# A state-space layer in a two-layer decoder trunk: issuing engines, order of loads and places of background products, on one core

## The chip, the core and the metric

The kernel runs on one core of a Trainium2 chip. A core has five engines that run side by side, each with its own instruction queue: TensorE (PE; its weight loads are shown as PEld), VectorE (DVE), ScalarE (ACT), GpSimd (POOL) and SyncE (SP), which here only issues DMA transfers. ACT and GpSimd can issue transfers too. An engine works its queue in order, so an instruction that waits holds up all that stand behind it. The metric is device time in microseconds of one execution; lower is better.

## The reference, cut to what matters

The model is a trunk of two layers for one sequence of 512 positions and 1024 channels in float32. Layer 0 mixes positions with attention, layer 1 with the state-space model below; each is followed by a gated feed-forward part. The shifts, scales and gates of every sub-layer come from a conditioning vector `c` by products with `w_mod`.

```
def s5_ssm(h, ...):                       # 64 groups of 16 channels, 64 complex states each
    u = h @ w_in
    bu = einsum('gph,bsgh->bsgp', b_bar, u in groups)
    _, states = associative_scan(combine, (lam_bar, bu), axis=1)   # over the 512 positions
    y = einsum('ghp,bsgp->bsgh', c_mat, states).real + d_skip * u
    z = gelu(y)
    g = z * sigmoid(z @ w_glu + b_glu)
    return g @ w_o
```

The result is multiplied by a gate and added to `x`; then comes a norm, whose shift and scale are again rows of `c_act @ w_mod + b_mod`.

## The kernel before

**Precision.** Matmuls run on pairs: a float32 tile is split into a rounded high half (a copy on ACT, `L163` for weights) and the remainder (a subtraction on VectorE, `L164`). `mm3` (`L169`, `L172`, `L173`) makes high x high, low x high and high x low, three matmuls for each 128x128 block of weights with 512 columns.

**Weights.** `load_w` takes 512 KB of weights from memory to a raw tile (three buffers, tag `wraw`), then splits it into one of `NW` = 5 pairs of buffers. The raw buffer comes free when the low half is made, the pair when the last matmul that reads it is done.

**Order of the instructions.** The program is written in one order, and a planner that estimates durations sets the order in each engine's queue when the kernel is built. Three things bind it: `tc.keep_in_program_order` (called `pe_pin` here, or `pinned=True` for gemvs) holds an instruction to the order of the program on its engine; `tc.issue_after` (in `behind_head` and `follow`) puts what is issued in a block behind a named instruction of the same engine; `follow("P", ...)` makes a chain of transfers on SP in this way. The planner also hands each transfer one of a small number of completion slots.

**Modulation in the background.** The 96 rows of the modulation are products of a 128x1024 piece of `w_mod` with `c_act` on VectorE (`gemv_step`, `L196`; its load on SP, `L195`, 512 KB into one of two `wg` buffers). Each is two rows of the profile, the product and a read of its accumulator. `bg(n)` issues the next `n`. Before the feed-forward part of layer 1 begins, all but the last 24 must be done; 18 are issued within the state-space layer.

**The state-space layer** (`ssm`). The 1024 channels are eight blocks of 128. For each block: eight units of `mm3` make `u` (`u_units`); ACT copies it to `ut` (`L1152`) and writes it to the DRAM tile `sU` (`L1153`, 256 KB in pieces of 256 bytes), from where it is read back in another layout as tile `u` (`L1155`). Four tables per block, made earlier, lie in DRAM: B (`pB`, 512 KB), R (`pR`, 256 KB), T and C (`pT`, `pC`, 512 KB each), with two buffers for each. `st_scan(bi)` multiplies `u` with B on PE (`pv`, 32 small matmuls), turns the result by R, scans it and turns it back on VectorE (eight to ten operations, `L1188` to `L1197`), and ACT copies the states to `st` (`L1202`). `st_out(bi)` makes `py` from u, T, `st` and C on PE (32 small matmuls) and ACT copies it to `yn` (`L1215`). `st_tr(bi)` transposes `yn` on PE (`pz`, `L1220`) and ACT applies gelu to give `z` (`L1223`).

A stage `s_` from 2 to 9 holds `st_out(s_-2)`, `st_scan(s_)` while there are blocks, two dense units, `st_tr(s_-2)`, and the rest of the dense units. The dense units are block 7 of `u` in stage 2, and then for each block `k` = `s_-3` the product of `z` of that block with the first five column blocks of `w_glu` (`glu_units`, weights `wglk`, 320 KB each), into five PSUM banks. PE's order here is that of the program.

After the stages PE makes the sixth column block (`g5`, weights `wgl`), the last block's units, and the seventh and eighth column blocks. Gating follows for each of the eight: sigmoid on ACT (`L1299`), times `z` on VectorE (`L1300`), split into `gzH` (ACT, `L1303`) and `gzL` (VectorE, `L1304`).

`out_proj` multiplies with `w_os`: two tiles are begun without the last of the eight gated blocks; the first five tiles are whole, each followed by its residual on VectorE (`L353`), a square on ACT (`L242`), a sum of squares on VectorE (`L243`) and the hook `after`; the last three tiles go in halves of 256 columns, and between the second halves PE makes the statistics of the first half (`stat`, `L264`) at a fixed place. In the same time the first four weights of the next part (`uph`) are loaded and split.

## Time and profile before

| | us |
|---|---|
| median of three timed runs | 1196.93 |
| their range | 1194.94 to 1197.47 |
| the profiled execution | 1194.65 |
| its span, first to last instruction | 1192.7 |
| its mean granted TensorE clock | 0.991 of full speed |

The profile is one execution on the chip. Its rows give the start in us, the duration, the engine, the line of the kernel, the operation and its tiles (output <- inputs), how many rows were merged, and in brackets how long the engine idled before it and what released it. A release is inferred; where the engine named had been done for long, it was something else, often a transfer. `SPq` and `ACTq` are issues of transfers. In the 10 us windows from 640 to 790 us, which hold the state-space layer, PE is busy for 8.8 to 10.0 of 10, VectorE for 4.4 to 9.4, ACT for 2.9 to 9.8, GpSimd for none, and the DMA engines for 0.20 to 1.03 of their time.

### The profile page before, as it was taken

What the parts mean: (1) busy time and instruction counts of PE and PEld (TensorE: products, weight loads), DVE (VectorE), ACT (ScalarE), POOL (GpSimd) and SP (SyncE); (2) the same over time, 40 slices, a digit from 0 to 9 for tenths busy, and PEclk for the clock granted to TensorE, in tenths of its full rate; (3) what the DMA queues carried; (4) which work ended last, traced back from release to release, by engine and by line L of the source; (5) the groups of instructions that cost most, each with busy time, mean ns of one, the idle gap of its engine ahead of it and who ended that gap; (6) DMA issues with size and microseconds to landing.
All of it is one profiled execution on the core that took longest, in us unless ns stands there. A gap on an engine that the chain in (4) does not pass through costs nothing.

```text
span 1192.7 us, 16459 instructions
## 1 busy us (share of the span) xinstructions
PE 1168.8 (98%) x6218; PEld 964.4 (81%) x6218; DVE 885.8 (74%) x1312; ACT 563.7 (47%) x893; POOL 270.4 (23%) x245
## 2 busy tenths in 40 slices
PE   8999999999999999989999999999999999999997
PEld 6887677699787878768889887879888888888887
DVE  6978988565999489888868598787598467744555
ACT  6756667456443134413336577646554134422443
POOL 1000000000298899998710000000000000000003
PEclk8999999999999999989999999999999999999999
DMA  8875653231348567778755598762166437442222
GB/s 301 316 262 165 203 179 109 90 121 54 89 142 273 177 215 222 207 233 294 247 153 182 182 322 288 246 224 77 53 216 225 124 118 188 153 124 71 83 76 71
DMA packets 92002, 211.00 MB, mean 177 GB/s; under 512 B 19602, under 2 KB 37906, under 8 KB 91923
## 3 DMA queue, kind: packets, MB, share of 16 engines
q1 hardware_dynamic: 83026, 205.76, 53.9%
q10 hardware_dynamic: 8320, 2.10, 0.8%
q0 software_dynamic: 576, 2.10, 0.5%
q8 instruction: 48, 0.79, 0.3%
q14 instruction: 32, 0.25, 0.1%
HBM read 188.68 MB, written 21.24 MB: 176 GB/s over the span
## 4 chain that ended last, share of the span: by engine, by line
PE 70%; POOL 8%; DVE 8%; DMA 7%; ACT 3%; issue 2%; SPq 1%; POOLq 0%; ACTq 0%; DVEq 0%
PE up L169 9%; PE up L172 9%; PE up L173 9%; PE dn L172 5%; PE dn L169 5%; PE dn L173 5%; PE o L772 2%; DVE ca L459 1%; PE t L754 1%; PE k L169 1%; PE q L169 1%; PE wo L169 1%; PE q L172 1%; PE q L173 1%; PE wo L173 1%
## 5 line engine op out<-in xcount | busy, mean ns | idle before, releaser
L173 PE MATMUL up<-hH,up_l 128*128 128x512 f32 x640 | 249.3, 390 | 1.1 <-DVE up_l L164 1.1
L169 PE MATMUL up<-hH,up_h 128*128 128x512 f32 x640 | 249.5, 390 | 0.0
L172 PE MATMUL up<-hL,up_h 128*128 128x512 f32 x640 | 249.3, 390 | 0.0
L459 DVE SCALAR_TENSOR_TENSOR ca<-up,small,ca 128x511 f32<-128x511 f32 (+1 forms) x176 | 131.4, 746 | 84.2 <-ACT ca L457 81.4
L196 DVE SCALAR_TENSOR_TENSOR wg<-wg,cact 128x1024 f32<-128x1024 f32 x96 | 122.8, 1294 | 40.1 <-DMA wg<-in_w_modT_dram 39.9
L172 PE MATMUL dn<-gL,dn_h 128*128 128x512 f32 (+1 forms) x394 | 145.9, 370 | 3.4 <-DVE gL L474 3.4
L169 PE MATMUL dn<-gH,dn_h 128*128 128x512 f32 (+1 forms) x394 | 146.3, 372 | 2.1 <-ACT gH L473 2.1
L173 PE MATMUL dn<-gH,dn_l 128*128 128x512 f32 (+1 forms) x394 | 145.7, 370 | 0.0
L173 PEld LDWEIGHTS up<-hH,up_l 128*128 128x128 f32 x640 | 120.1, 188 | 26.9 <-DVE up_l L164 2.0
L169 PEld LDWEIGHTS up<-hH,up_h 128*128 128x128 f32 x640 | 120.1, 188 | 26.0 <-issue 1.2
L172 PEld LDWEIGHTS up<-hL,up_h 128*128 128x128 f32 x640 | 120.1, 188 | 24.4
L1368 POOL TENSOR_SCALAR xa<-x,Anorm_out 128x256 f32<-128x256 f32 x7 | 5.7, 815 | 573.7 <-ACT dn_h L163 558.9
L163 ACT ACTIVATE up_h<-up_r 128x1024 fp32r<-128x1024 f32 x80 | 84.2, 1053 | 104.7 <-PE dn L172 48.0
L164 DVE TENSOR_TENSOR up_l<-up_r,up_h 128x1024 fp32r<-128x1024 f32 x80 | 121.9, 1524 | 10.1 <-ACT up_h L163 9.2
L457 ACT ACTIVATE ca<-up,small 128x512 f32<-128x512 f32 x88 | 67.7, 770 | 90.3 <-PE up L173 90.3
L172 PEld LDWEIGHTS dn<-gL,dn_h 128*128 128x128 f32 x394 | 75.1, 191 | 16.3 <-DVE gL L474 4.0
L169 PEld LDWEIGHTS dn<-gH,dn_h 128*128 128x128 f32 x394 | 75.0, 190 | 15.9 <-ACT gH L473 3.0
L173 PEld LDWEIGHTS dn<-gH,dn_l 128*128 128x128 f32 x394 | 75.0, 190 | 12.4
L353 DVE SCALAR_TENSOR_TENSOR x<-dn,mod,x 128x512 f32<-128x512 f32 (+1 forms) x55 | 37.3, 679 | 61.6 <-PE dn L173 61.6
L163 ACT ACTIVATE dn_h<-dn_r 128x1024 fp32r<-128x1024 f32 (+1 forms) x48 | 46.7, 981 | 55.9 <-PE dn L172 28.0
L466 ACT ACTIVATE ca<-ca 128x512 f32<-128x512 f32 x44 | 27.8, 632 | 91.7 <-DVE ca L459 89.9
L164 DVE TENSOR_TENSOR dn_l<-dn_r,dn_h 128x1024 fp32r<-128x1024 f32 (+1 forms) x48 | 62.8, 1308 | 8.3 <-ACT dn_h L163 8.1
(324 smaller groups left out, 2352.2 us busy)
## 6 DMA issues: line engine op xcount, KB each, us to landing
wg<-in_w_modT_dram SPq DMA_DIRECT2D x96, 512.0 KB
up_r<-in_w_up_dram SPq DMA_DIRECT2D x80, 512.0 KB
dn_r<-in_w_down_dram SPq DMA_DIRECT2D x32, 512.0 KB
wgs<-in_w_modT_dram SPq DMA_DIRECT2D x16, 512.0 KB
dn_r<-in_w_down_dram SPq DMA_DIRECT2D x16, 384.0 KB
wv_r<-in_w_v_dram SPq DMA_DIRECT2D x8, 512.0 KB
wk_r<-in_w_qk_dram SPq DMA_DIRECT2D x8, 512.0 KB
wq_r<-in_w_qk_dram SPq DMA_DIRECT2D x8, 512.0 KB
```

What stands on the lines that cost most here:

```text
L163: order("S", lambda: S.activation(wh[:, :n], raw[:, :n], AF.Copy))
L164: pin["split"] = order("V", lambda: V.tensor_tensor(wl[:, :n], raw[:, :n], wh[:, :n].bitcast(F32), ALU.subtract))
L169: ins = PE.matmul(ps, ah, bh, start=start, stop=False)
L172: PE.matmul(ps, ah, bl, start=False, stop=False)
L173: PE.matmul(ps, al, bh, start=False, stop=stop)
L196: mul = lambda: V.scalar_tensor_tensor(w, w, 1.0, cact, ALU.mult, ALU.mult, accum_out=raw[:, col:col + 1])
L353: add = lambda: V.scalar_tensor_tensor(xs, pv, gate, xs, ALU.mult, ALU.add)
L457: follow("S", lambda: S.activation(ca, ps, AF.Identity, bias=small[:, cb:cb + 1], scale=tapw[2]))
L459: follow("V", lambda: V.scalar_tensor_tensor(ca[:, q:], ps[:, :T - q], tapw[2 - q], ca[:, q:], ALU.mult, ALU.add))
L466: follow("S", lambda: S.activation(cg, cg, AF.Silu))
L754: ins = PE.transpose(pt[:, c:c + P], wts[pr][h2][i][:, j * P:(j + 1) * P], ident)
L772: ins = PE.matmul(po[pr][h2 * HD:(h2 + 1) * HD, j * P:], vn[:, j, hd:hd + HD], src, start=j == 0, stop=j == 3)
```

## The change

- The eight loads of `u` are issued by GpSimd instead of SP.
- The tables are asked for one by one (`load_tab`) in the chain on SP: in stage `s_` R of block `s_+1`, T and C of `s_`, B of `s_+2` (before: B and R of `s_+1`, then T and C of `s_`). The load of the GLU weights of block `s_-1` (`glu_load`) joins the chain behind them; before, the planner placed these loads. The weights of `g5` are loaded behind the last of the chain.
- The loads of `w_in` for blocks 4 to 7 stand together ahead of their units (`u_load`).
- Splitting `z` of block `s_-2` and the GLU weights of that block (`glu_split`) stands at the end of stage `s_`, with VectorE's two subtractions held to the program's order; before, it stood in stage `s_+1`, not held.
- A one-column gelu (`warm`) on ACT right behind the last norm tile brings the gelu table.
- Gemvs: three behind the last split of `w_in` ahead of the stages, two in stage 8 and one after stage 9 (before: four in each of the two, not held); none after the last two gating tiles (before: two after each); up to two instead of one behind each whole tile of the output projection.
- The gating tile `sg` has four buffers instead of two.
- `load_w` gets an argument `chain`, false by default.

```diff
-                def load_scan(bi):
-                    ...
-                def load_out(bi):
-                    ...
+                SRC = {"B": (sB, [P, 2, 512]), "R": (sR, [P, 2, 256]), "T": (sT, [P, 8, P]), "C": (sC, [P, 8, P])}
+                def load_tab(bi, which):
+                    for g in which:
+                        src, shape = SRC[g]
+                        if bi < 8:
+                            t = blk[bi][g] = tp.tile(shape, F32, tag="p" + g, bufs=2, name="p" + g)
+                            follow("P", lambda: SP.dma_start(t.rearrange("p r n -> p (r n)"), src[bi].rearrange("p r n -> p (r n)")))
...
-                    pin["u"] = SP.dma_start(u.rearrange("p g c -> p (g c)"), sU[bi].rearrange("j (h g) c -> h j (g c)", g=8))
+                    G.dma_start(u.rearrange("p g c -> p (g c)"), sU[bi].rearrange("j (h g) c -> h j (g c)", g=8))
+                warm = np_.tile([P, 64], F32, tag="warm", bufs=1, name="warm")[:, 0:1]
+                with behind_head():
+                    S.activation(warm, ones[:, 0:1], AF.Gelu_apprx_tanh)
...
+                def u_load(bi):
+                    with behind_head(pin["head"][HEADW[bi - 4]]):
+                        uw[bi] = load_w(I["w_in"][bi * P:(bi + 1) * P, :], name=f"win{bi}")
...
                 def glu_units(k):
-                    with behind_head([u_loads]):
-                        w = load_w(I["w_gluk"][k * P:(k + 1) * P, :], n=NGLU * P, name=f"wglk{k}")
+                    w = gw_[k][1:]
+                    dense.extend(...)
+                def glu_load(k):
+                    if k < KD:
+                        w = [wp.tile([P, D], F32R if g else F32, tag=("wraw", "wH", "wL")[g], bufs=NW if g else 3, name=f"wglk{k}_{g}")[:, :NGLU * P] for g in range(3)]
+                        follow("P", lambda: SP.dma_start(w[0], I["w_gluk"][k * P:(k + 1) * P, :]))
+                        gw_[k] = w
+                def glu_split(k):
                     S.activation(zh[0][k], zf[k], AF.Copy)
-                    V.tensor_tensor(zh[1][k], zf[k], zh[0][k].bitcast(F32), ALU.subtract)
-                    dense.extend(...)
+                    pe_pin(V.tensor_tensor(zh[1][k], zf[k], zh[0][k].bitcast(F32), ALU.subtract))
+                    raw, wh, wl = gw_[k]
+                    S.activation(wh, raw, AF.Copy)
+                    pe_pin(V.tensor_tensor(wl, raw, wh.bitcast(F32), ALU.subtract))
...
+                for bi in range(4, 8):
+                    u_load(bi)
                 u_units(4)
                 u_units(5)
+                with behind_head([pin["split"]]):
+                    bg(3, False)
                 run(UPRE)
                 st_scan(0)
-                load_scan(2)
+                load_tab(2, "BR")
                 u_units(6)
                 run(USTG[0])
                 st_scan(1)
+                load_tab(3, "B")
+                glu_load(0)
                 u_units(7)
                 run(USTG[1])
...
                     if s_ < 8:
                         st_scan(s_)
-                    if s_ + 1 < 8:
-                        load_scan(s_ + 1)
-                    if s_ < 8:
-                        load_out(s_)
+                        load_tab(s_ + 1, "R")
+                        load_tab(s_, "TC")
+                        load_tab(s_ + 2, "B")
+                    glu_load(s_ - 1)
...
                     st_tr(s_ - 2)
-                    if s_ >= 8:
-                        with behind_head([pin["comb"]]):
-                            bg(4, False)
+                    if s_ == 8:
+                        bg(2)
                     run(100)
-                gw, g5 = glu_w(NGLU), bank(aux, name=f"glu{NGLU}")
+                    if s_ == 2:
+                        zh = new_h()
+                    glu_split(s_ - 2)
+                    if s_ == 9:
+                        bg(1)
+                with behind_head([line["P"]]):
+                    gw = glu_w(NGLU)
+                g5 = bank(aux, name=f"glu{NGLU}")
...
-                sg = gp.tile([P, T], F32, tag="sg", bufs=2, name="sgl")
+                sg = gp.tile([P, T], F32, tag="sg", bufs=4, name="sgl")
...
-                if mt >= len(gb):
-                    bg(2)
...
-            R = out_proj(..., after=lambda: bg(min(1, sum(q[0] is not None for q in bgq) - 24)), ...)
+            R = out_proj(..., after=lambda: bg(min(2, sum(q[0] is not None for q in bgq) - 24)), ...)
```

More of the change, by code (lines that the diff above doesn't have):

```diff
@@ L142, in follow, with load_w @@
         return line[eng]
-    def load_w(src, n=D, name="w", own=None, lined=False):
+    def load_w(src, n=D, name="w", own=None, lined=False, chain=False):
         raw = wp.tile([P, D], F32, tag="wraw", bufs=3, name=name + "_r")
@@ L160, in load_w @@
             wl = wp.tile([P, D], F32R, tag="wL", bufs=NW, name=name + "_l")
-        pin["load"] = SP.dma_start(raw[:, :n], src)
+        fetch = lambda: SP.dma_start(raw[:, :n], src)
+        pin["load"] = follow("P", fetch) if chain else fetch()
         order = follow if lined else lambda eng, fn: fn()
@@ L1305, in ssm @@
                 gz.append((gh, gl))
[L1306 to L1307 removed]
             acc2 = new_acc()
[L1309 removed]
+            R = out_proj(lambda mt: I["w_os"][mt * P:(mt + 1) * P, :], gz, mcol(1, 2, 0), acc2, "wos", perm=True, after=lambda: bg(min(2, sum(q[0] is not None for q in bgq) - 24)),
                          head=([up_src(1, q, s) for q in range(2) for s in range(2)], "uph"))
```

25 lines of the change are left out of this document (6 added, 19 removed).

## The prediction

> **What bounds the kernel now.** I read the page first, then the TensorE waits, then TensorE's timeline through the state-space (SSM) layer. The page has TensorE (PE) busy for almost the whole span, so the change can only win what PE waits in the stages that it touches.
>
> ```profile
> span 1192.7 us, 16459 instructions
> PE 1168.8 (98%) x6218; PEld 964.4 (81%) x6218; DVE 885.8 (74%) x1312; ACT 563.7 (47%) x893; POOL 270.4 (23%) x245
> ```
>
> The span is 1192.7 us, that execution took 1194.65, and the median of the three timed runs is 1196.93. I count savings in the span and subtract them from the median; the executions shown differ by up to 2.5 us among themselves.
>
> In the stage loop each stage begins with the output products `py` of block s-2. The starts of stages 3 to 9, and of what follows the loop, are in PE's timeline (start, duration, operation):
>
> ```profile
> 702.59 1.09 PE L1146 MATMUL py<-pT,u 128*64 128x128 f32 x16
> ...
> 710.34 1.09 PE L1146 MATMUL py<-pT,u 128*64 128x128 f32 x16
> ...
> 717.26 1.09 PE L1146 MATMUL py<-pT,u 128*64 128x128 f32 x16
> ...
> 724.20 1.09 PE L1146 MATMUL py<-pT,u 128*64 128x128 f32 x16
> ...
> 732.47 1.09 PE L1146 MATMUL py<-pT,u 128*64 128x128 f32 x16
> ...
> 740.03 1.09 PE L1146 MATMUL py<-pT,u 128*64 128x128 f32 x16
> ...
> 747.53 1.09 PE L1146 MATMUL py<-pT,u 128*64 128x128 f32 x16
> ...
> 753.42 0.39 PE L169 MATMUL glu<-hH,wgl_h 128*128 128x512 f32 x1
> ```
>
> Stages 3 to 7 hold the same PE work. Stage 4 takes 717.26-710.34 = 6.92 and stage 5 takes 6.94: that is PE without a wait. Stage 3 takes 7.75 (0.83 over), stage 6 8.27 (1.35 over), stage 7 7.56 (0.64 over). Stages 8 and 9 have no scan products; stage 9 takes 5.89, stage 8 7.50 (1.61 over). The places of these waits, and the two of the output projection `wos`, with the idle time in brackets:
>
> ```profile
> 707.67 0.66 PE L1220 MATMUL pz<-consts,yn 128*128 128x128 f32 x4 [0.59 <-ACT yn L1215]
> ...
> 727.29 1.15 PE L1146 MATMUL pv<-u,pB 128*64 128x64 f32 x32 [1.12 <-DVE wgl_l L164]
> ...
> 744.85 0.66 PE L1220 MATMUL pz<-consts,yn 128*128 128x128 f32 x4 [1.24 <-ACT yn L1215]
> ...
> 776.76 0.39 PE L172 MATMUL wos<-gzL,wos_h 128*128 128x512 f32 x1
> 776.99 0.39 PE L173 MATMUL wos<-gzH,wos_l 128*128 128x512 f32 x1
> 777.56 0.49 PE L169 MATMUL wos<-gzH,wos_h 128*128 128x512 f32 x1 [0.19 <-ACT gzH L1303]
> 778.93 0.50 PE L172 MATMUL wos<-gzL,wos_h 128*128 128x512 f32 x1 [0.88 <-DVE gzL L1304]
> ```
>
> Without a wait, matmuls start 0.23 apart (the first two `wos` rows); the next two start 0.57 and 1.37 apart, so 0.34 + 1.14 = 1.48 is lost. All together 0.83 + 1.35 + 0.64 + 1.61 + 1.48 = **5.91 us** can be won, and no more.
>
> **The change part by part.** *Gelu's table.* ACT loads it inside stage 2, and runs late from there to the `yn` that stage 3 waits for:
>
> ```profile
> 700.37 1.28 ACT L1223 ACT_TABLE_LOAD   x1
> ...
> 707.02 0.60 ACT L1215 ACTIVATE yn<-py 128x512 f32<-128x512 f32 x1
> ```
>
> The load goes behind the last norm tile, where ACT idles until u0 is complete. 1.28 against a wait of 0.83: the wait goes, +0.83. No other table is needed between (ACT only copies there).
>
> *Order of loads; u off SP.* In stage 6 `pv` is released by no VectorE result (`wgl_l` is no input of it); its table B, row 721.73, was issued late. SP stood still before it:
>
> ```profile
> 705.46 0.37 ACTq L1153 DMA_DIRECT2D sU<-ut  x1
> ...
> 712.05 0.58 SPq L1128 DMA_DIRECT2D pT<-sT  x1
> 720.85 0.32 SPq L1128 DMA_DIRECT2D pC<-sC  x1
> ...
> 721.73 0.38 SPq L1121 DMA_DIRECT2D pB<-sB  x1
> ...
> SPq L1128 <- DMA sU<-ut: 8.2, 1, 8.2
> ```
>
> The load of pC shares no data with the write of sU, issued at 705.46; SP waited 8.2 us for that write all the same, as for a completion slot in use. Everything behind (B, the rotation table R, u) then came in one burst, so stages 6 and 7 waited, stage 7's scan came late, and stage 8 with it. In the new order B is asked for one stage earlier, u takes no place in SP's queue, and six of the eight GLU loads no longer crowd in ahead of the write. The slot itself stays: C of stage 4 is still about the eighth transfer after the last sU write, so the wait shrinks and does not go. B of block 6 follows it directly. Before, that load took 727.29 - 721.73 = 5.6 to arrive, and `pv` of stage 6 will be due at 724.20 - 0.83 + 2 = 725.4; so the write has to be done by some 719, two us sooner than before. I think it is, and credit 1.35 + 0.64 = 1.99 of stages 6 and 7.
>
> *VectorE's order in a stage; z and weight splits behind the scan.* The scan's end, and so ACT's `st`, comes one subtraction earlier. In stage 8 `yn` stood right behind this row, which ends at 744.18:
>
> ```profile
> 742.50 1.68 ACT L1202 ACTIVATE st<-m 64x252 f32<-64x252 f32 x4 [1.27 <-DVE m L1197]
> ```
>
> 1.61 goes, but stage 8 has no `pv` to cover the split of block 5, now due behind the scan: at most one subtraction, 0.60 by the row of acc below; taken 0.3. The loads of w_in for blocks 4 to 7, listed earlier, were done by then anyway: nothing. `chain` in `load_w` is used by nobody: nothing. The first of the last three GLU weights is now loaded behind the last table, where its low half was made in stage 6 before (`wgl_l` at 727.29). Its buffer comes free with the split of block 5, early in stage 8, so from 740.03 - 2.82 = 737.2 to some 740; PE needs it when stage 9 ends, 753.42 - 4.43 = 749.0. Load and split have 9 us: hidden, with a few us to spare.
>
> *u by GpSimd.* The nearest price is GpSimd's own transfer of sR in an earlier phase (issue 0.8 us, 512 KB each; u has 256), against u0's issue and the first scan product:
>
> ```profile
> 678.96 4.56 SPq L1155 DMA_DIRECT2D u<-sU  x3
> ...
> 682.83 1.15 PE L1146 MATMUL pv<-u,pB 128*64 128x64 f32 x32
> ...
> DMA to landing us min/median/max: 3.4/3.5/4.3
> ...
> 684.03 0.69 DVE L1188 TENSOR_TENSOR m<-pv,pR 128x512 f32<-128x512 f32 x1 [6.76 <-PE pv L1146]
> ```
>
> 678.96 + 3.5 = 682.46 is in time, + 4.3 = 683.26 is 0.43 late; below, nothing is won, since PE did not wait. Taken 0.2. GpSimd's own queue is empty here, so nobody stands behind it; later u's have a stage or more. [...]
>
> *Three gemvs behind the last w_in split.* They take 1.14 each on VectorE (below) in the 6.76 that it idles, last row above; their three loads (1.5 MB) land among the first u transfers. Free while the first scan keeps its slack of several us; taken 0.3 for the shared DMA.
>
> *Gating.* Four gemvs leave it, five leave stages 8 and 9, and four buffers let the sigmoids run ahead: the 1.48 goes.
>
> *Output projection.* Eighteen gemvs must be done before the next layer's modulation; 2+3+2+1 are placed earlier, so ten stay for five tiles, two behind each tile. Before, the window held eight (x16 counts accumulator reads too), four of them ahead of the first residual:
>
> ```profile
> 766.00:812.00 46.00, 9.79 (x16) 1.00 0.70 226
> ...
> 784.29 1.23 DVE L196 SCALAR_TENSOR_TENSOR wg<-wg,cact 128x1024 f32<-128x1024 f32 x1 [2.51 <-DMA wg<-in_w_modT_dram]
> ...
> 786.98 1.28 DVE L353 SCALAR_TENSOR_TENSOR x<-wos,mod,x 128x512 f32<-128x512 f32 x1
> ...
> 804.13 0.69 DVE L243 TENSOR_TENSOR acc<-acc,sq 128x512 f32<-128x512 f32 x1
> 804.73 1.22 DVE L196 SCALAR_TENSOR_TENSOR wg<-wg,cact 128x1024 f32<-128x1024 f32 x1
> ...
> 805.87 1.18 DVE L353 SCALAR_TENSOR_TENSOR x<-wos,mod,x 128x512 f32<-128x512 f32 x1
> 806.97 1.22 DVE L164 TENSOR_TENSOR uph_l<-uph_r,uph_h 128x1024 fp32r<-128x1024 f32 x1
> ...
> 812.73 0.42 DVE L243 TENSOR_TENSOR acc<-acc,sq 128x256 f32<-128x256 f32 x1 [0.54 <-ACT sq L242]
> ...
> 785.00 0.39 PE L173 MATMUL wos<-gzH,wos_l 128*128 128x512 f32 x1
> ...
> 813.53 0.50 PE L264 MATMUL stat<-ones,acc 128*128 128x1 f32 x4
> ...
> 820.76 0.28 PE L173 MATMUL up<-hH,uph_l 128*128 128x256 f32 x1
> ```
>
> The last sum of squares ends at 813.15 and `stat` on PE, whose place is fixed, starts 0.38 later: VectorE is the close second here. PE has tile 0 at 785.00 + 0.39 = 785.4, so VectorE may use 813.53 - 785.4 = 28.1. It will need ten gemvs at 1.14 (804.73 to 805.87), 11.4; five residuals at 1.10 (805.87 to 806.97), 5.5; four sums at 0.60, 2.4; three splits of `wos` and four of `uph` at 1.2, 8.4; and for the three last half tiles a residual and a sum each, some 1.0 by the row of 0.42, 3.0. That is 30.7: 2.6 too many. A split of `uph` whose buffer comes late falls behind `stat`; with one or two of them 1.4 or 0.2 remain. Ends: 0.2 and 2.6, more if loads are late (rivals). I take **1.5 us of new PE wait before `stat`**.
>
> Sum: 5.91 - 0.3 - 0.2 - 0.3 - 1.5 = 3.6, so a span of 1189.1 and a median of **1193.3**.
>
> **The rivals.** (1) *VectorE fits*: the `uph` splits fall behind `stat`, no new wait; 5.91 - 0.8 = 5.1, 1191.8. For it: PE uses them from some 820 on (row 820.76). Against: they are ready at the same time.
>
> (2) *The stages stay late*: the sU write holds SP as long as before, and only the table and gating terms come, 0.83 + 1.48 less 1.5: 0.8, 1196.1. For it: the same eight-transfer distance, and 1.5 MB of gemv loads moved ahead of it. Against: less is queued.
>
> (3) *Slower*: the gemvs are kept behind the sums before them, and each pair has its loads issued only when the pair before is done. The row at 784.29 waited 2.51 for such a load. If two of the four later pairs wait so, VectorE is 2.6 + 5.0 = 7.6 late at `stat`: 5.1 - 7.6, 1199.4. It decides once the wait before `stat` is over 5.1.
>
> [...]
>
> (5) *Not as said*: what is not pinned is ordered by the planner's clock, and new order elsewhere eats the gain: 1196.9.
>
> **How the numbers follow.** Forecast 0.45 (own range 1191.3 to 1195.0), (1) 0.17, (2) 0.17, (3) 0.13, (4) 0.03, (5) 0.05. A measurement tells about 0.2% (2.4 us) from no change. Faster: most of the forecast (0.37), all of (1), a little of (2), 0.57. Slower: most of (3) and little else, 0.13. Same: 0.30. The range 1190.2 to 1199.0 takes in (1) with the spread of runs and reaches into (3).
>
> **What would show it.** Right: stages 3 to 7 all near 6.92, stage 8 near 6.2, no table load after 690, no SP wait of 8 us for sU, no wait at the first `wos` tile, a wait of 0.2 to 2.6 before `stat` that VectorE's sum releases. Wrong: `pv` of block 0 waiting for u by over 0.5; the g5 products waiting for wgl5; `stat` more than 3 late, or not at all.

## The result and the profile after

| | before | after |
|---|---|---|
| median of the timed runs, us | 1197.15 (4 runs) | 1210.56 (4 runs, 1206.63 to 1214.04) |
| ratio after / before, with 95% interval | | 1.0119 (1.0092 to 1.0146) |
| profiled execution, us | 1194.65 | 1206.63 |
| its span, us | 1192.7 | 1204.5 |

The changed kernel is 1.2% slower. The forecast was 1193.3 us with a range up to 1199.0; the time lies 11.6 us above that range. Line numbers of the changed kernel differ by a few from those of before; the names are the same.

TensorE's waits within the state-space layer (what waited <- what ended it: us in all, times, longest):

```profile
PE glu L174 <- DVE wgl_l L165: 3.5, 1, 3.5
PE stat L265 <- DVE acc L244: 3.3, 1, 3.3
PE pv L1143 <- issue: 2.6, 1, 2.6
PE glu L170 <- ACT wgl_h L164: 0.4, 1, 0.4
PE glu L174 <- DVE wglk L1263: 0.2, 1, 0.2
...
PE pz L1221 <- ACT yn L1216: 0.2, 1, 0.2
```

The waits of before that the prediction counted are gone or down to 0.2: those for `yn`, for B and for `gz`. (The row left out is a wait of 0.2 for `hL` at the start of the layer, which both kernels have.) In their place stand three that before did not have, at `pv` of block 0, at the sixth GLU product and at `stat`: 2.58 + (0.44 + 3.53) + 3.31 = 9.9 us. The span grew by 11.8, although the stages became shorter, so the waits alone are not the whole loss. To see the rest, TensorE's timeline is cut at five landmarks: the statistics that open the layer, the first `py`, `pz` of block 7, the first product of `out_proj`, and the second `rbc` in it. Before, then after:

```profile
645.08 0.17 PE L264 MATMUL stat<-ones,acc 128*128 128x1 f32 x1
...
694.29 0.33 PE L1146 MATMUL py<-pT,u 128*64 128x128 f32 x2
...
750.91 0.27 PE L1220 MATMUL pz<-consts,yn 128*128 128x128 f32 x1
...
773.14 0.39 PE L169 MATMUL wos<-gzH,wos_h 128*128 128x512 f32 x1
...
827.71 0.38 PE L286 MATMUL rbc<-dg,ones 128*128 128x256 f32 x1
```

```profile
644.72 0.17 PE L265 MATMUL stat<-ones,acc 128*128 128x1 f32 x1
...
698.08 0.33 PE L1143 MATMUL py<-pT,u 128*64 128x128 f32 x2
...
752.09 0.27 PE L1221 MATMUL pz<-consts,yn 128*128 128x128 f32 x1
...
780.43 0.39 PE L170 MATMUL wos<-gzH,wos_h 128*128 128x512 f32 x1
...
839.49 0.38 PE L287 MATMUL rbc<-dg,ones 128*128 128x256 f32 x1
```

Segment by segment, after minus before: to the first `py` 53.36 - 49.21 = +4.15; the stage loop 54.01 - 56.62 = **-2.61**; the sixth GLU product and what follows 28.34 - 22.23 = +6.11; `out_proj` 59.06 - 54.57 = +4.49. Together +12.1. In each of the three segments that lost, the loss is larger than its wait. Why, the granted clock shows, in windows behind the three waits (PEclk is the third number from the end):

```profile
685.00:690.00 5.00, 4.88 (x42) 4.25 (x43) 2.83 (x6) 0.60 (x1) 1.04 (x2) 0.66 0.98 282
760.00:765.00 5.00, 5.00 (x15) 4.00 (x16) 2.21 (x2) 1.06 (x1) 0.00 (x0) 0.66 1.03 325
...
825.00:830.00 5.00, 5.00 (x29) 4.95 (x29) 1.46 (x5) 0.38 (x1) 0.00 (x0) 0.66 0.19 71
```

TensorE is busy in these windows and gets 0.66 of its clock; in before it is 1.00 in every window from 640 to 850 us. That is the second part of the loss: from the first `pv` to the second 6.89 - 5.39 = 1.50 us, behind the GLU product 6.11 - 3.97 = 2.1, at and behind `stat` 4.49 - 3.31 + 1.48 = 2.7 (the last with the 1.48 of the gating, which was won): some 6.3 us in all, in which the slower start behind a wait is counted too (the product behind the wait of 0.44 is followed 0.34 us later, that behind 3.53 after 0.38, where the others of the GLU product at full clock stand 0.23 apart). So the three places cost 9.9 + 6.3 = 16.2 us, and the stage loop and the gating won 4.1.

The stage loop did what was forecast for its first five stages:

```profile
706.38 1.09 PE L1143 MATMUL py<-pT,u 128*64 128x128 f32 x16
...
713.32 1.09 PE L1143 MATMUL py<-pT,u 128*64 128x128 f32 x16
...
727.18 1.09 PE L1143 MATMUL py<-pT,u 128*64 128x128 f32 x16
...
734.10 1.09 PE L1143 MATMUL py<-pT,u 128*64 128x128 f32 x16
...
741.07 1.09 PE L1143 MATMUL py<-pT,u 128*64 128x128 f32 x16
...
748.35 1.09 PE L1143 MATMUL py<-pT,u 128*64 128x128 f32 x16
...
754.59 0.39 PE L170 MATMUL glu<-hH,wgl_h 128*128 128x512 f32 x1
```

Stage 3 takes 6.94, stages 4 and 5 together 13.86, stage 6 6.92, stage 7 6.97. Stage 8 takes 7.28 (7.50 before) and stage 9 6.24 (5.89 before): nothing was won there.

### The profile page after: what moved, and what is told of

The parts are those of the page before. It is cut to its first block, busy times and chain, and to the rows that moved or that the text cites. A ratio compares the mean times of both kernels' runs of the same rounds, so it can differ in the third digit from the quotient of the medians.

```text
span 1204.5 us, 16456 instructions
## 1 busy us (share of the span) xinstructions
PE 1174.6 (98%) x6218; PEld 968.8 (80%) x6218; DVE 875.2 (73%) x1312; ACT 562.7 (47%) x894; POOL 273.4 (23%) x253
## 4 chain that ended last, share of the span: by engine, by line
PE 73%; POOL 10%; DVE 6%; DMA 4%; ACT 3%; issue 2%; SPq 0%; POOLq 0%; DVEq 0%; ACTq 0%
PE up L170 9%; PE up L173 9%; PE up L174 9%; PE dn L170 5%; PE dn L173 5%; PE dn L174 5%; PE o L773 2%; PE t L755 1%; PE k L170 1%; PE u L173 1%; PE u L170 1%; PE u L174 1%; PE q L170 1%; PE wo L170 1%; PE k L173 1%
## 5 line engine op out<-in xcount | busy, mean ns | idle before, releaser
L165 DVE TENSOR_TENSOR up_l<-up_r,up_h 128x1024 fp32r<-128x1024 f32 x80 | 114.5, 1431 | 15.4 <-ACT up_h L164 14.4
```

The source lines that it names most:

```text
L165: pin["split"] = order("V", lambda: V.tensor_tensor(wl[:, :n], raw[:, :n], wh[:, :n].bitcast(F32), ALU.subtract))
```

## The experiments

Each is the changed kernel with a small edit, but for e13, which is the kernel before. The ratio is to the kernel before, run on the same chip between them. The intervals of e1 to e6, each with two of the three losses or more left in, overlap with the changed kernel's, so there the segments of one profile carry the argument; those of e7, e8, e9 and e12 do not overlap with it. The four segments are those above, in us against before's first profile; a minus is a gain.

| | ratio (95%) | to first py | stage loop | GLU | out_proj | layer |
|---|---|---|---|---|---|---|
| the change | 1.0119 (1.0092 to 1.0146) | +4.1 | -2.6 | +6.1 | +4.5 | +12.1 |
| e1 u by SyncE | 1.0083 (1.0055 to 1.0110) | -0.1 | -2.6 | +7.0 | +5.0 | +9.3 |
| e2 early gemvs moved | 1.0101 (1.0059 to 1.0143) | +0.7 | -1.1 | +7.1 | +5.3 | +12.1 |
| e3 wgl5 first | 1.0069 (1.0044 to 1.0093) | +4.7 | -0.9 | 0.0 | +4.9 | +8.7 |
| e4 one gemv a tile | 1.0085 (1.0055 to 1.0114) | +6.4 | -2.4 | +7.5 | -1.7 | +9.8 |
| e5 gemvs without loads | 1.0108 (1.0085 to 1.0131) | -0.1 | 0.0 | +6.0 | +1.5 | +7.5 |
| e6 TensorE kept busy | 1.0105 (1.0074 to 1.0135) | +6.2 | -2.3 | +5.0 | +2.3 | +11.2 |
| e7 three mended | 1.0007 (0.9990 to 1.0024) | +0.2 | -1.4 | 0.0 | -0.7 | -1.9 |
| e8 same, u of 4 to 7 by GpSimd | 1.0013 (0.9995 to 1.0031) | +0.1 | -2.0 | 0.0 | +0.8 | -1.1 |
| e9 splits placed by hand | 1.0011 (0.9991 to 1.0030) | -0.1 | -0.8 | +1.6 | -1.7 | -0.9 |
| e10 gelu not ahead | one time | +6.7 | -2.5 | +6.9 | +4.9 | +15.9 |
| e11 two gating buffers | one time | +6.2 | -2.1 | +6.8 | +4.5 | +15.4 |
| e12 third gemv out | 0.9987 (0.9967 to 1.0007) | 0.0 | -3.4 | 0.0 | -1.0 | -4.4 |
| e13 before again | one time | 0.0 | -1.9 | 0.0 | +0.5 | -1.3 |
| e14 e12 again | one time | 0.0 | -1.9 | 0.0 | -1.5 | -3.4 |

The start of the layer lies between 641.85 and 649.28 us in these profiles, with no edit ahead of it; the kernel before alone has 645.08 and 647.59. That spread is in every time, and the segments are free of it.

### Who makes u late: e1, e2, e5

e1 undoes the issuing engine:

```
-                    G.dma_start(u..., sU[bi]...)
+                    SP.dma_start(u..., sU[bi]...)
```

> The changed kernel with one thing undone: SyncE issues the loads of u again, as before the change; the three early gemvs stay. In the changed kernel pv of block 0 waits 2.58 us for u and the landmarks of TensorE lose about 4 us there. Theory Q (the queue: GpSimd's path is what makes u late, 5.7 us from issue to landing for block 0): u of block 0 lands in 2 to 3 us, the wait at pv is under 0.5 us and 4 us come back; SyncE's wait for a slot behind the u loads returns and costs up to 2 us in stages 6 and 7, so 1206 to 1209 us. Theory C (contention: u's transfer shares the DMA engines with the gemv loads, whoever issues it): u still takes over 4 us from issue, the wait stays over 1.5 us, and the time is 1210 us or more with the slot wait on top (1212). The waits of 3.5 us ahead of the GLU product and 3.3 us ahead of the statistics stay under both.

`pv` of block 0 no longer waits, and the stage loop keeps all of its gain (-2.6). So taking u off SyncE is not what won in the stages: SyncE's longest wait of a table load for a write of `sU` is 1.7 us in e1, against 8.2 in before. That the new order of the table loads did it is argued and not shown, as no run undoes that order alone; and how much was won at all, e13 below puts in doubt. But e1 doesn't separate queue from contention, as its issues show. The changed kernel's and then e1's (start, time over the merged rows, queue):

```profile
678.08 1.49 SPq L196 DMA_DIRECT2D wg<-in_w_modT_dram  x2
...
679.37 1.16 POOL L1153 DMA_DIRECT2D u<-sU  x2 [77.60 <-DMA sU<-ut]
```

```profile
673.62 1.47 SPq L196 DMA_DIRECT2D wg<-in_w_modT_dram  x2
680.46 0.58 SPq L1153 DMA_DIRECT2D u<-sU  x1
681.13 0.54 SPq L196 DMA_DIRECT2D wg<-in_w_modT_dram  x1
```

In the changed kernel two gemv loads of 512 KB go out just ahead of u0 (two more had been used by then); in e1 the third goes out only behind u0, since both stand in one queue. The queue that u left had also kept gemv loads behind it.

e2 moves the gemvs and leaves u on GpSimd:

```
-                with behind_head([pin["split"]]):
-                    bg(3, False)
...
                 gz.append((gh, gl))
+                if mt >= 5:
+                    bg(1)
```

> The changed kernel with the three early gemvs moved to the gating (one after each of its last three tiles), u still loaded through GpSimd. Two gemv loads of 512 KB, those of stage 8, are still issued beside u's. Theory C (contention with the gemv loads): u of block 0 lands in about 3 to 4 us, pv waits under 1 us, and 3 to 4 us come back: 1206 to 1208 us. Theory Q (GpSimd's path): the landing stays near 5.7 us, the wait over 2 us, and the time within 1 us of the changed kernel's, 1210. A third theory, L (VectorE's multiplications of the gemvs hold up GpSimd's issue), gives what C gives here, and is told from it by a run that keeps the loads without the multiplications. The waits ahead of the GLU product and the statistics stay.

The wait fell to 0.68, and u0 landed 3.7 us after its issue began (5.7 in the changed kernel):

```profile
683.73 1.15 PE L1143 MATMUL pv<-u,pB 128*64 128x64 f32 x32 [0.68 <-issue]
```

No gemv load was issued in the 6 us before u0 here. Contention or VectorE, then. The layer as a whole gained nothing here: the stage loop gave back 1.5 (waits for `yn` of 1.4), and `stat` waited 4.3 in place of 3.3; neither was followed up. e5 lets VectorE multiply without the loads:

```
-                    bg(3, False)
+                    bg(3, False, load=False)      # multiplies cact by itself
```

> The changed kernel in which the three early gemvs multiply without their loads (the vector by itself, in place of the weights), so that three of the modulation values are not the reference's. VectorE does the same three multiplications at the same place; 1.5 MB of loads are gone. With those gemvs moved away altogether, u of block 0 landed 3.15 us after its issue ended (5.08 in the changed kernel) and pv waited 0.7 us (2.58). Theory C (the loads fill the DMA engines): the same here, a landing of 3.0 to 3.4 us, a wait under 1 us, the ratio to before about 1.010. Theory L (VectorE's multiplications hold GpSimd's issue or its descriptors): landing 4.5 us or more, wait 2 us or more, ratio 1.012.

u0 again landed in 3.7 us, and `pv` did not wait at all. All three multiplications stood beside the transfer here (679.54 to 683.05, the transfer from 679.68 to 683.4), more than in the changed kernel, where two were done before u0's issue. VectorE's multiplications are innocent; **the loads of the early gemvs made u late**, by 2.0 us (5.7 to landing), and in the other five profiles with u on GpSimd and these loads by more: 6.4 in e3 and e11, 6.5 in e4, 6.8 in e6 and 6.9 in e10, with waits at `pv` of 3.3 to 3.8. The changed kernel's own profile shows this loss at its smallest.

The rest of the 2.58, about what e2 still waits (0.68), comes ahead of the read. From the issue of the write to the issue of the read it took 679.37 - 673.77 = 5.60, and on SyncE in before 678.96 - 674.14 = 4.82. ScalarE waits for the same write, to use `ut` again, and so shows when it was done. Rows of after, then of before:

```profile
673.77 0.38 ACTq L1150 DMA_DIRECT2D sU<-ut  x1
...
678.88 0.60 ACT L1149 ACTIVATE ut<-u 128x512 f32<-128x512 f32 x1 [3.23 <-DMA sU<-ut]
```

```profile
674.14 0.38 ACTq L1153 DMA_DIRECT2D sU<-ut  x1
...
678.98 0.60 ACT L1152 ACTIVATE ut<-u 128x512 f32<-128x512 f32 x1 [2.96 <-DMA sU<-ut]
```

The read's issue on GpSimd comes 0.49 behind ScalarE's row, and on SyncE 0.02 ahead of it; e1 to e6, e10 and e11 have the same 0.49 or 0.02. The other 0.27 is the write's. In e5 the write, too, was done 2.4 us sooner (679.19 - 676.48 = 2.71), as no gemv loads stood ahead of it, so its missing wait is not the landing's alone.

e5's ratio is larger than its layer (+7.5 us) lets expect. Its profiled execution had a mean granted clock of 0.994, and the three others 0.990 or 0.991: they may have had the half clock behind `stat` that this one lacks (see the last section), but they left no profile.

### The sixth GLU weight: e3

The chain in the changed kernel, on VectorE's timeline, and the row of ScalarE's that it could have followed:

```profile
756.14 0.69 DVE L1260 TENSOR_TENSOR hL<-z,hH 128x512 fp32r<-128x512 f32 x1 [5.14 <-ACT hH L1259]
756.75 0.82 DVE L1263 TENSOR_TENSOR wglk<-wglk,wglk 128x640 fp32r<-128x640 f32 x1
757.49 1.22 DVE L197 SCALAR_TENSOR_TENSOR wg<-wg,cact 128x1024 f32<-128x1024 f32 x1
...
758.63 2.35 DVE L165 TENSOR_TENSOR wgl_l<-wgl_r,wgl_h 128x1024 fp32r<-128x1024 f32 x2
```

```profile
747.96 1.06 ACT L164 ACTIVATE wgl_h<-wgl_r 128x1024 fp32r<-128x1024 f32 x1
```

The low half of wgl5 is made at 758.63 on VectorE, though ScalarE (last row) had made its high half at 749.0. VectorE idled for 5.14 us in between, in front of hL of block 7, which is pinned to the program's order and waits for the last gelu; the last split of `wglk` and the gemv of stage 9 stood ahead of it too. e3 puts the split ahead of them:

```
+                    if s_ == 9:
+                        with behind_head([line["P"]]):
+                            gw = glu_w(NGLU)
                     glu_split(s_ - 2)
...
-                with behind_head([line["P"]]):
-                    gw = glu_w(NGLU)
```

> The changed kernel with the sixth GLU weight (wgl5) loaded and split ahead of the pinned splits of stage 9, not behind them. Theory O (order: its split on VectorE stands behind hL of block 7, which waits 5.14 us for its input, though its own input was there 9.6 us before): the waits of 0.44 and 3.53 us at the GLU product go, with the half clock behind them; the first product of out_proj comes 5 to 6 us earlier, and the time is 1204 to 1206 us. Theory D (VectorE is simply short of time there: the split only changes places with others that are needed as much): another wait of 2 us or more appears in stage 9 or ahead of the products of block 7, and the time stays above 1208 us. The waits at pv of block 0 and at the statistics stay under both.

The 6.1 us are gone, clock and all. Some 1.7 came back in the stage loop, 1.1 of it in stage 9, which is neither 0 nor theory D's 2. hH of block 6 began 2.1 us behind the end of the gelu that it needs (752.36 against 750.29), and in the changed kernel 1.0 (748.93 against 747.93): ScalarE's half of wgl5's split stood between in both, but in e3 it waited 0.49 for its load, and a split of `wglk` stood there as well. TensorE waited in many small steps:

```profile
PE glu L170 <- ACT hH L1259: 0.8, 2, 0.4
PE glu L174 <- DVE wglk L1263: 0.5, 2, 0.2
PE glu L173 <- DVE hL L1260: 0.4, 2, 0.2
```

### The pairs of gemvs: e4

```
-  after=lambda: bg(min(2, sum(...) - 24))
+  after=lambda: bg(min(1, sum(...) - 24))
...
-                        bg(1)            # stage 9
+                        bg(2)
+                if mt >= 6:              # gating
+                    bg(2)
```

> The changed kernel with one gemv after each of out_proj's first five tiles, as before the change, not two; the other five go to stage 9 (one) and to the last two tiles of the gating (two each). Theory G (the pairs of gemvs, each waiting for its 512 KB load, hold the residual sums and with them acc and the statistics): the wait of 3.31 us ahead of stat falls below 1 us, its half clock goes, and the time is 1204 to 1206 us; some 1.5 us may come back as a wait in the gating, as it was before. Theory R (the sums are late for another reason: weight splits on VectorE or the squares on ScalarE): stat still waits over 2 us and the time stays within 1.5 us of 1210. A fourth gemv in stage 9 may lengthen the wait at the GLU product by 1.2 us.

The wait at `stat` is gone, and `out_proj` is 1.7 us shorter than before's. In the changed kernel VectorE was full; from the first residual to the last sum that `stat` needs:

```profile
790.84 1.28 DVE L354 SCALAR_TENSOR_TENSOR x<-wos,mod,x 128x512 f32<-128x512 f32 x1 [6.12 <-PE wos L174]
...
819.53 1.23 DVE L197 SCALAR_TENSOR_TENSOR wg<-wg,cact 128x1024 f32<-128x1024 f32 x1 [1.09 <-DMA wg<-in_w_modT_dram]
...
821.01 1.22 DVE L197 SCALAR_TENSOR_TENSOR wg<-wg,cact 128x1024 f32<-128x1024 f32 x1
...
822.16 0.42 DVE L244 TENSOR_TENSOR acc<-acc,sq 128x256 f32<-128x256 f32 x1
```

That is 822.58 - 790.84 = 31.7 us with 1.09 of it a wait for a load. Behind 790.84 TensorE left 819.32 - 790.84 = 28.5 us for it, so VectorE was late by what it had too much, 2.2, and by that wait for a load, 1.09. The four gemvs in the gating cost no wait there, with four gating buffers; the gemv added to stage 9 (the fourth of stages 8 and 9) lengthened the GLU wait to 4.7, as expected.

### The clock: e6

```
+                for q in range(16):
+                    pe_pin(PE.matmul(g5, wk(gw, 0)[0], zh[0][0], start=True, stop=True))
...
+        for q in range(12):              # ahead of stat
+            pe_pin(PE.matmul(R["ps"][:, 256:256 + P], ones, ones, start=True, stop=True))
```

> The changed kernel with work that is thrown away put into two of TensorE's waits: 16 repeats of the sixth GLU product's first matmul (some 0.23 us each) ahead of the wait for the split of wgl5, and 12 matmuls of 128x128 into unused columns of the statistics' bank ahead of the wait for acc. Neither wait ends earlier by this. Theory H (the granted clock falls because TensorE was idle): the clock of 0.83 behind the first wait and of 0.66 behind the second become 1.00, the work behind them takes 1.6 to 2 us and 2.7 us less, so the ratio to before falls from 1.012 to about 1.008. Theory P (the clock falls for another reason, such as the load on the memory or on the other engines at that time): the clock stays under 0.9 in both windows, and the ratio at 1.012. The wait at pv of block 0, left as it is, keeps its half clock.

The clock stayed at full behind both places, where windows of this length had shown 0.66 (the wait at the GLU product ended at 767.29 here, that at `stat` at 828.80):

```profile
767.00:772.00 5.00, 4.71 (x21) 3.88 (x22) 2.59 (x3) 1.06 (x1) 0.00 (x0) 1.00 1.01 360
...
830.00:835.00 5.00, 5.00 (x42) 4.94 (x42) 3.38 (x13) 1.74 (x4) 0.00 (x0) 1.00 0.34 103
```

So in these two places the idle time is the cause of the half clock, not the other engines' load. `out_proj` took back 2.2 us, all of it behind `stat`; the GLU segment only 1.1, since the wait there, fillers and all, was 16 x 0.23 + 1.1 = 4.8 in this execution in place of 3.97. `pv`, left alone, waited 3.6 in place of 2.58 and kept its half clock, so the layer is only 0.9 us shorter than the changed kernel's. The ratio of 1.0105 does not tell theory H from theory P; the clock in the windows does.

### Are gelu's table and the buffers worth anything: e10, e11

```
-                with behind_head():
-                    S.activation(warm, ones[:, 0:1], AF.Gelu_apprx_tanh)      # e10
...
-                sg = gp.tile([P, T], F32, tag="sg", bufs=4, name="sgl")         # e11
+                sg = gp.tile([P, T], F32, tag="sg", bufs=2, name="sgl")
```

> The changed kernel without the instruction that has gelu's table loaded ahead. The prediction put 0.83 us of the stage loop to it. Theory T (the table load of 1.28 us is on the path at the first gelu): from the first py to the last pz the kernel is 1.6 to 2.0 us shorter than before's, in place of 2.62, and a wait of 0.8 us is back in stage 3. Theory F (the stages have slack there once tables and VectorE's work are in order): 2.3 us or more, no new wait. The three losses stay, so the single time says little: 1206 to 1214 us.

The table load is back inside stage 2, and the stage loop is as short as with it ahead: theory F, in one execution. Stage 3, from the `py` at 708.78 to that at 715.72, takes 6.94:

```profile
704.03 1.28 ACT L1221 ACT_TABLE_LOAD   x1
```

> The changed kernel with two gating buffers, as before the change; no gemv is in the gating in either. The prediction put the wait of 1.48 us at out_proj's first tile to the buffers and the four gemvs of the gating together. Theory B (the buffers): a wait of 1 us or more for gz is back at the first tile, and from there to the statistics the kernel loses that much against the changed one. Theory M (the gemvs in the gating were the cause): the wait is under 0.4 us. Its time says little: 1206 to 1214 us.

With two buffers, too, there is no wait for `gz` (theory M). With four buffers and four gemvs in the gating (e4) there is none either. Only with the two together, as in before, was the wait of 1.48 there, so either half of the change seems enough. In e4 and e11, though, TensorE had stood still for 4 to 5 us just ahead of the gating, which gave VectorE and ScalarE time. For the buffers, e7 and e12 below show the same without that pause (four buffers, gemvs in the gating, no wait for `gz`); for two buffers with no gemvs no run shows it.

### Mended together: e7, e8, e9, e12

e7 takes the edits of e1, e3 and e4, with five gemvs in the gating (1, 2 and 2 behind its last three tiles) in place of the one more in stage 9.

> The changed kernel with the three places mended together: u issued by SyncE, wgl5 loaded and split ahead of the splits of stage 9, one gemv after each of out_proj's first five tiles and five gemvs after the last three tiles of the gating. If the three losses are separate and their mends add up (0.36, 0.50 and 0.34% of the time when done singly, the last with 1.2 us more from a gemv that is not added to stage 9 here), the ratio to before is 0.998 to 0.996, that is 2 to 5 us faster than before; what the change does in the stage loop (2.5 to 3 us) is then what is left of it. If VectorE's work or the loads only collide elsewhere, a new wait of 2 us or more appears in the gating or at the statistics, and the ratio stays above 1.001.

The three waits are gone and the layer is 1.9 us shorter than before's, but the time is not: 1.0007. The stage loop, at -1.4, lost in stage 9 what e3 lost there (4.9 us to the last `pz`, 3.7 in the changed kernel). e8 tries GpSimd for the later u's:

```
+                    (SP if bi < 4 else G).dma_start(u..., sU[bi]...)
```

> As the mended kernel, but GpSimd issues the loads of u of blocks 4 to 7 (SyncE those of blocks 0 to 3, which TensorE awaits at once). Theory S (in the stages, SyncE's wait behind u delays the tables of the next block): stages 5 to 7 are 0.5 to 2 us shorter in sum than with all of u on SyncE, and the ratio 0.1% lower. Theory N (the order of the table loads already took that wait away, so who issues u no longer matters there): the sum of the stages differs by less than 0.4 us and the ratios agree within their intervals.

-2.0 in place of -1.4 in the stage loop, and 1.5 the other way in `out_proj`; the ratios agree. By the spread that e13 and e14 show below, 0.6 is no finding: theory N is not contradicted. e9 places both halves of wgl5's split by hand and moves two more gemvs into VectorE's idle time:

```
+                    if s_ == 9:
+                        line["S"] = pin["yn"]
+                        gw = load_w(I["w_glu"][0:P, :], name="wgl5", lined=True, chain=True)
+                        bg(2)
                     glu_split(s_ - 2)
...
-                        bg(2)            # stage 8
+                        bg(3)
```

> The mended kernel (u by SyncE, one gemv after each tile of out_proj), with the sixth GLU weight's two splits placed by hand: ScalarE's behind the last yn, VectorE's ahead of hL of block 7; and two more gemvs taken out of the gating into VectorE's idle time of stages 8 and 9 (three in stage 8, two ahead of hL of block 7), so that the gating has one after each of its last three tiles. In the mended kernel ScalarE's split of that weight (1.06 us) stood ahead of hH of block 6, and stage 9 waited 0.94 us for hH, hL and wglk. Theory W (that place was all that was wrong with stage 9): those waits go, the stage loop is 2.2 to 2.7 us shorter than before's (1.38 in the mended kernel), the product for wgl5 waits under 0.3 us, and the state-space layer is 3 to 4.5 us shorter than before's; ratio 0.9965 to 0.999. Theory V (VectorE and the loads have no room left there): a gemv waits for its load ahead of hL of block 7 and a wait of 1 us or more appears in stage 9 or at wgl5; ratio 1.000 to 1.003.

Theory V came: a gemv waited for its load and held hL of block 6 behind it.

```profile
748.68 1.22 DVE L197 SCALAR_TENSOR_TENSOR wg<-wg,cact 128x1024 f32<-128x1024 f32 x1 [4.03 <-DMA wg<-in_w_modT_dram]
...
749.83 0.69 DVE L1260 TENSOR_TENSOR hL<-z,hH 128x512 fp32r<-128x512 f32 x1
```

TensorE waited 2.13 for it, and had 0.50 of its clock afterwards (753 to 756 us). e12 goes back to `bg(2)` in stage 8, with one gemv behind each of the gating's last four tiles.

> The kernel before it without the third gemv of stage 8, which waited 4.03 us for its load and held hL of block 6: two gemvs in stage 8, wgl5's splits placed by hand, two gemvs ahead of hL of block 7, one after each of the last four tiles of the gating, one after each of out_proj's first five, u by SyncE. If the third gemv was all that went wrong (theory W still), stage 9 waits under 0.5 us in all, the stage loop is 2.2 to 2.7 us shorter than before's, and the state-space layer 3 to 4.5 us shorter; ratio 0.9965 to 0.999. If stage 9 has no room for the two gemvs either (theory V), a wait of 1 us or more stays there and the ratio is 1.000 or more. The time at which the layer starts varies by several us among the profiled executions, so the layer's own length tells more than one time.

TensorE's waits in the layer are then one row, beside the 0.2 at its start:

```profile
PE glu L174 <- DVE wglk L1263: 0.2, 1, 0.2
```

The layer is 4.4 us shorter than before's first profile, and the ratio 0.9987 (0.9967 to 1.0007): at best a little faster, and not shown to be.

### Is the yardstick steady: e13, e14

> The kernel before the change, profiled a second time, as a control of the profile against which the segments of all others are measured. If that profile is typical, its segments come out within 0.5 us: from the first scan product to the first py, from there to the last pz, to the first product of out_proj, to the statistics. If the waits in before's stages vary by themselves, the sum of these segments is 1.5 us or more shorter, and so much less of the mended kernel's 4.4 us is a gain. The start of the layer may lie up to 6 us apart in either case. Time 1189 to 1199 us.

It is not. From one profile of before to the other the stage loop differs by 1.9 us; stage 3 takes 6.96 in the second and waits for nothing:

```profile
705.09 1.09 PE L1146 MATMUL py<-pT,u 128*64 128x128 f32 x16
...
712.05 1.09 PE L1146 MATMUL py<-pT,u 128*64 128x128 f32 x16
```

> The last of the mended kernels, profiled a second time on the chip on which before is profiled again. Its layer was 4.44 us shorter than before's, while the times of 12 runs gave a ratio of 0.9987 (0.9967 to 1.0007), some 1.6 us. If the layer's gain is steady and the rest is the varying start of the layer, the segments repeat within 0.5 us. If a wait comes and goes in the mended kernel (VectorE and the loads are nearly full there), one of 1 us or more shows up in stage 9, at the gating or at the statistics. Time 1187 to 1197 us.

In e14 a wait of 1.7 for `yn` came up in stage 7, which e12 did not have. The mended layer is thus 3.4 to 4.4 us shorter than before's first profile, and before's own second profile 1.3: on the mean of two and two some 3.9 - 0.7 = 3.2 us, 0.27%, which the interval of e12's ratio (down to -0.33%) allows. The three losses, some 4 to 7 us each, were there in every profile in which their cause was left in, and stand clear of this spread, with one exception: behind e5's wait at `stat` there was no half clock. The gain of 2.6 in the stage loop does not stand clear of it.

## Why the prediction was wrong, point by point

The forecast for the layer was -3.6; the profile shows +12.1. The difference of 15.7 lies in four steps, and within three of them in one thing that no step had, the half clock. The three steps that made the kernel slower are u with the early gemvs, wgl5, and `stat`.

**u by GpSimd, taken 0.2, and the early gemvs' loads, taken 0.3: measured 4.15** (a wait of 2.58, with the clock behind it; 4.7 to 6.7 in the other profiles that have both). They were priced apart. The row of sR (3.4 to 4.3 us) was the right price for u with few loads beside it: 3.7 in e2 and e5. With two gemv loads just ahead it was 5.7, and up to 6.9 in the other profiles. The step asked who stands behind u in GpSimd's queue, and not what GpSimd's transfer would no longer stand in front of once it left SyncE's.

**wgl5, "hidden, with a few us to spare": measured 6.1.** The step counted buffer, load and split, and for ScalarE's half that held: it was done at 749.0, 5.6 us ahead of its first product (754.59). The step left out VectorE's order. The low half was due behind a pinned instruction that waits for the last gelu, and so could not come before 756.8, whenever its data came; it came at 758.63.

**`stat`, taken 1.5: the wait measured 3.3, with the clock 6.0.** The sum of VectorE's work, 30.7, was right (31.7, of which 1.09 a wait for a load), and its end of 2.6 was near. The wrong choice was that one or two `uph` splits would fall behind `stat`: all four were made before it. Rival (3), pairs that wait for their loads, is in it with 1.09, where it had 5.0.

**The stage loop, forecast -4.1: measured -2.6 against the first profile and -0.8 against the second.** Stages 3 to 7 came out at 6.92 to 6.97 as forecast. Two terms were wrong. Gelu's table (0.83) is worth nothing in the changed kernel (e10), and the wait that it was to remove was absent in before's second execution. Stages 8 and 9 were to win 1.3 and won nothing: the wait for `yn` in stage 8 fell from 1.24 to 0.17, but one of 0.24 for `wglk` is new, and the first products of the stage start 0.62 and 0.73 us apart (before 0.35 and 0.25). SyncE's wait of 8.2 us for the write is gone, but not by u's move (e1).

**The gating, 1.48: right.** The buffers alone give it (e4, e7, e12); the gemvs' move alone did in e11, with the pause ahead of the gating.

**The half clock, not in the sum at all: some 6.3 us** of the 16.2 that the three places cost. Of the waits shown in before, none was longer than 1.24 us and none was followed by it, so the prediction had no row for it. The shortest waits that had it behind them are 2.13 us (e9) and 2.58 (the changed kernel); the last section has more on it.

The prediction's own list of what would show it wrong held the three places, `pv` of block 0, the GLU products and `stat`, each as a sign only. Rival (3) had a price for `stat`, and nothing had one for wgl5.

## What to carry to other kernels

In these runs a gap of over 2 us on TensorE cost its length and, but for one (e5), more with the half clock behind it: 1.5 to 2.7 us at the three places of the changed kernel. Behind a wait of 1.67 us (e14) the clock stayed at 1.00, so one long wait cost more than several short ones of the same sum. When a transfer is moved to another engine's queue, ask what it had kept behind it in the old one; when a piece of work is moved, look for the pinned instruction in front of its new place and what that one waits for. And profile the kernel before twice ahead of counting its waits as winnable: here 1.9 us of 4.4 were gone in a second execution.

## What the runs showed of the hardware that was not expected

TensorE's granted clock fell to one half behind waits of 2.13 (0.50 in e9's window from 753 to 756 us), 2.58, 3.31 and 3.58 us. It stayed at 1.00 behind waits of up to 1.67 us (e14, windows from 733 to 739 us), and behind a wait of 2.94 us in e5:

```profile
823.33 0.61 PE L266 MATMUL stat<-ones,acc 128*128 128x1 f32 x4 [2.94 <-DVE acc L245]
```

```profile
825.00:830.00 5.00, 5.00 (x43) 4.95 (x42) 3.41 (x11) 2.21 (x5) 0.00 (x0) 1.00 0.26 97
```

So the length of the wait alone doesn't decide. More can be read from windows of 1 us. In the changed kernel, behind the GLU wait:

```profile
760.00:761.00 1.00, 1.00 (x3) 0.82 (x4) 0.98 (x1) 0.00 (x0) 0.00 (x0) 0.59 1.27 348
...
763.00:764.00 1.00, 1.00 (x5) 0.81 (x4) 0.71 (x1) 0.00 (x0) 0.00 (x0) 0.70 0.88 356
```

The two windows between them have 0.50. A mean of 0.59 is 0.82 us at one half, so the half clock began at 760.18; 0.70 is 0.60 us of it, so it ended at 763.60. Worked out in this way, it had these starts and lengths in the layer:

| | starts, us | lengths, us | distances |
|---|---|---|---|
| the change | 685.08, 760.18, 821.62 | 3.4, 3.4, 6.8 | 75.10 = 22 x 3.414, 61.44 = 18 x 3.413 |
| e10 | 685.44, 760.54, 825.40 | 6.8, 6.8, 6.8 | 75.10 = 22 x 3.414, 64.86 = 19 x 3.414 |
| e11 | 688.30, 763.40, 828.24 | 6.8, 6.8, 6.8 | 75.10 = 22 x 3.414, 64.84 = 19 x 3.413 |
| e5 | 760.74 | 3.4 | 249.18 = 73 x 3.413 from a start at 511.56, ahead of the layer |

Within each of these executions the starts thus lie whole steps of 3.41 us apart, and each stretch lasts one or two steps. Where the steps fall differs from one execution to the next: the first starts of the change, e10 and e11 lie 0.36 and 2.86 us apart. As an estimate from these distances, with the steps taken as lines at which the clock can change, e5 fits: with lines at 760.74 and 18 steps later, 822.18, the idle time at `stat` (820.4 to 823.3) was cut into 1.8 us before the line and 1.2 behind it. In e11 the idle time at `stat` (825.7 to 828.7) had 2.6 of its 3.0 us ahead of the line at 828.24, and the clock halved there. How much idle time between two lines it takes, if that is what decides, is not settled: 1.4 and 0.2 us between 749.19 and 752.60 were followed by the half clock in e9, and 1.67 in e14 and 1.8 in e5 were not.

At 0.50 of the clock, a stretch of 3.4 or 6.8 us costs half of it at most, 1.7 or 3.4 us, less half of what TensorE idles in it: an estimate from the lengths in the table.

u0's transfer of 256 KB through GpSimd took 3.7 us from issue to landing with no gemv load issued just before it (e2, e5), and 5.7 to 6.9 with two (in the changed kernel 1.3 and 0.1 us ahead). It was issued 0.5 us later behind the write that it waits for than one on SyncE (0.49 behind ScalarE's row for that write, against 0.02 ahead of it).
